# Moving the second-last group's store from the GpSimd queue to the SP queue

## The chip, the cores and the metric

The kernel runs on one core of a Trainium2 chip. The metric is device time in microseconds, as the median of several executions; lower is better. A kernel counts as faster or slower here when it moves by more than 2%.

## The reference, cut to what matters

```python
batch, heads, seq, dim = 8, 12, 512, 64          # Q, K, V float32
Q_feat = np.maximum(0, Q) + 1
K_feat = np.maximum(0, K) + 1
KV = np.einsum('bhkd,bhkv->bhdv', K_feat, V)
K_sum = np.sum(K_feat, axis=2)
numerator = np.einsum('bhqd,bhdv->bhqv', Q_feat, KV)
denominator = np.einsum('bhqd,bhd->bhq', Q_feat, K_sum)
return numerator / (denominator[:, :, :, None] + 1e-10)
```

Three inputs and one output of 12.58 MB each: 50.33 MB have to cross between HBM and the core.

Of the kernel before, what the change touches and what calls it, by code (L numbers as in the profile page):

```python
# [20 lines left out]
def kernel(  # L21
# [23 lines left out]
    NG = NPAIR // NP  # L45
# [57 lines left out]
    def store(g):  # L103
        o_sb = outs.pop(g)
        o_to = o_dram[:, g * NP : g * NP + NP]
        if g < NG - 1:
            nc.gpsimd.dma_start(out=o_to, in_=o_sb)  # L107
            return
        for h in range(2):
            nc.sync.dma_start(out=o_to[:, h:NP:2], in_=o_sb[:, h:NP:2])  # L110
# [83 lines left out]
    with tc.manual_schedule():  # L194
# [36 lines left out]
        for g in range(NG - 1):  # L231
            if g:
                k_features(g)
                q_features(g)
                transposes(g - 1)
            if g >= 2:
                output(g - 2)
            keys_values(g)
            if g + AHEAD < NG:
                load_k(g + AHEAD)  # L240
                load_v(g + AHEAD)
                load_q(g + AHEAD)
            if g >= LAG:
                store(g - LAG)
# [9 lines left out]
        for g in range(last - LAG, NG):  # L254
            store(g)
# [30 lines left out]
```

## The kernel before: the parts the change touches

The work is cut into `NG = 12` groups. For each group the kernel loads K, V (in four pieces) and Q over the GpSimd queue, with a cast from float32 to bfloat16, and stores one output tile of 1 MB. `h` counts the two halves in which a group's output is computed; each half covers every second of the four blocks of the tile.

```python
def store(g):
    o_sb = outs.pop(g)
    o_to = o_dram[:, g * NP : g * NP + NP]
    if g < NG - 1:
        nc.gpsimd.dma_start(out=o_to, in_=o_sb)
        return
    for h in range(2):
        nc.sync.dma_start(out=o_to[:, h:NP:2], in_=o_sb[:, h:NP:2])
# ... (cut: loads, features, matmuls, output)
for g in range(NG - 1):
    # ... (cut: compute of the groups, loads three groups ahead)
    if g >= LAG:                      # LAG = 3
        store(g - LAG)
last = NG - 1
# ... (cut: compute of the last groups)
for g in range(last - LAG, NG):       # groups 8, 9, 10, 11
    store(g)
```

## Time and profile before

| | before |
|---|---|
| time, median of 3 runs | 129.26 us (129.12 to 129.71) |
| span in the profile | 127.4 us |
| busy: PE, DVE, GpSimd, ACT | 57%, 52%, 43%, 37% |
| DMA engines | full from about 3 us to 123 us |
| HBM traffic | 50.33 MB, 395 GB/s over the span |

No compute engine is near its limit, while the DMA engines have no gap. The page's part on DMA issues tells how deep the queue is. Its columns are what is moved, the issuing queue, the count, the size of each, and the median time from issue to landing in us:

```profile
out_dram<-o_sb POOLq DMA_DIRECT2D x11, 1024.0 KB, 12.0
...
out_dram<-o_sb SPq DMA_DIRECT2D x2, 512.0 KB, 5.9
```

A store of 1 MB needs about 2.6 us on 16 engines, yet lands 12.0 us after its issue. Most of the other 9 us it waits behind older transfers.

### The profile page before, as it was taken

The page shows a single profiled execution, that of the slowest core. Times are in us where ns is not written, and L with a number is a line of the kernel's source. Part 1 is how long each engine was busy: PE and PEld are TensorE (multiplying, and loading weights), DVE is VectorE, ACT ScalarE, POOL GpSimd, SP SyncE. Part 2 cuts the span into 40 slices and gives each one's busy share as a digit, 9 for nine tenths or more (in the row PEclk, how much of TensorE's full clock was granted, in tenths as well). Part 3 has the DMA queues.
Part 4 walks back from the last instruction along what each step waited for, and adds up shares of the span by engine and source line. Part 5 has one row for each costly group of instructions (what it writes and reads, how often), then busy time and mean ns, then how long its engine had stood idle before and what let it go on. Part 6 is the DMA issues. An engine that isn't in the chain of part 4 may idle for free.

```text
span 127.4 us, 2373 instructions
## 1 busy us (share of the span) xinstructions
PE 72.6 (57%) x960; PEld 53.0 (42%) x960; DVE 66.1 (52%) x155; ACT 47.1 (37%) x76; POOL 54.3 (43%) x92
## 2 busy tenths in 40 slices
PE   0000099819259691994903992991993896956000
PEld 0000077618146471674702661771662664834000
DVE  4898802086292855919309507705714825779300
ACT  7940006942800927055550054046028009190000
POOL 6695775617346164544442462282273240202000
PEclk9999999999986999599996577568559559996555
DMA  4999999999999999999999999999999999999980
GB/s 89 329 210 210 207 205 208 211 210 208 211 206 214 206 210 214 206 328 256 208 292 293 206 268 321 206 242 344 210 222 353 220 209 371 421 412 421 403 327 2
DMA packets 13914, 32.13 MB, mean 252 GB/s; under 512 B 1360, under 2 KB 1360, under 8 KB 13904
## 3 DMA queue, kind: packets, MB, share of 16 engines
q0 software_dynamic: 13088, 29.89, 99.6%
q1 hardware_dynamic: 816, 2.10, 4.7%
q8 instruction: 7, 0.11, 0.3%
q14 instruction: 3, 0.02, 0.0%
HBM read 37.75 MB, written 12.58 MB: 395 GB/s over the span
## 4 chain that ended last, share of the span: by engine, by line
DMA 61%; DVE 12%; PE 8%; POOL 7%; issue 5%; POOLq 0%
DMA q_raw<-in_Q_dram 33%; DMA k_raw<-in_K_dram 18%; DMA out_dram<-o_sb 10%; DVE o_sb L184 9%; PE kva_ps L141 5%; POOL v_blk L93 5%; PE qt_ps L160 2%; DVE recip L183 2%; PE o_ps L173 1%; POOL q_raw L100 1%; DVE qf L116 1%; POOL k_raw L86 1%; DVE kf L116 1%; POOL zero L195 0%; POOLq L93 0%
## 5 line engine op out<-in xcount | busy, mean ns | idle before, releaser
L141 PE MATMUL kva_ps<-v_blk,kf 128*64 128x320 bf16 x384 | 41.5, 390 | 15.7 <-DMA v_blk<-in_V_dram 15.7
L141 PEld LDWEIGHTS <-kf 128*64 128x64 bf16 x384 | 28.1, 145 | 25.0 <-DVE qf L116 15.7
L173 PE MATMUL o_ps<-kva_diag,qt 128*64 128x130 bf16 x384 | 20.9, 249 | 29.8 <-DVE o_sb L184 29.2
L93 POOL DMA_DIRECT2D v_blk<-in_V_dram x48 | 26.5, 556 | 26.4 <-DMA k_raw<-in_K_dram 12.8
L184 DVE TENSOR_TENSOR o_sb<-o_ps,recip 128x512 f32<-128x512 f32 x48 | 33.2, 691 | 1.6
L151 ACT CAST kva_diag<-kva_ps 64x256 bf16<-64x256 f32 x24 | 8.9, 372 | 66.2 <-PE kva_ps L141 65.9
L161 ACT COPY qt<-qt_ps 128x1024 bf16<-128x1024 bf16 x24 | 29.6, 1301 | 0.3
L173 PEld LDWEIGHTS <-qt 128*64 128x64 bf16 x384 | 13.8, 122 | 35.7 <-DVE o_sb L184 33.9
L116 DVE TENSOR_SCALAR qf<-q_raw 128x1024 bf16<-128x1024 bf16 x24 | 9.2, 426 | 33.6 <-DMA q_raw<-in_Q_dram 33.6
L107 POOL DMA_DIRECT2D out_dram<-o_sb x11 | 8.5, 771 | 22.5 <-DMA q_raw<-in_Q_dram 8.2
L116 DVE TENSOR_SCALAR kf<-k_raw 128x1024 bf16<-128x1024 bf16 (+1 forms) x24 | 10.9, 495 | 9.8 <-DMA k_raw<-in_K_dram 9.8
L160 PE MATMUL qt_ps<-identity,qf 128*128 128x128 bf16 x192 | 13.8, 229 | 0.0
L160 PEld LDWEIGHTS <-qf 128*128 128x128 bf16 x192 | 11.8, 103 | 4.2 <-issue 4.0
L183 DVE RECIPROCAL recip<-o_ps 128x8 f32<-128x8 f32 x48 | 9.5, 197 | 5.2 <-PE o_ps L173 5.2
L86 POOL DMA_DIRECT2D k_raw<-in_K_dram x11 | 7.8, 713 | 8.5 <-DVE recip L183 5.2
L100 POOL DMA_DIRECT2D q_raw<-in_Q_dram x12 | 8.8, 730 | 4.6 <-DMA v_blk<-in_V_dram 2.1
L152 ACT CAST kva_diag<-kva_ps 64x4 bf16<-64x4 f32 x24 | 4.0, 168 | 0.0
L206 DVE MEMSET v_blk<- 128x2925 f32 x1 | 2.5, 2496 | 0.7 <-DVE ones L202 0.7
L224 DVE MEMSET v_blk<- 128x2925 f32 x1 | 2.5, 2496 | 0.6 <-issue 0.6
L212 DVE MEMSET v_blk<- 128x2925 f32 x1 | 2.5, 2496 | 0.6 <-issue 0.6
L219 POOL MEMSET kva_diag<- 128x520 bf16 x3 | 2.0, 719 | 0.0
L207 ACT COPY v_blk<-zero 128x2195 f32<-128x2195 f32 x1 | 2.0, 2019 | 0.0
(15 smaller groups left out, 7.9 us busy)
## 6 DMA issues: line engine op xcount, KB each, us to landing
out_dram<-o_sb POOLq DMA_DIRECT2D x11, 1024.0 KB, 12.0
q_raw<-in_Q_dram POOLq DMA_DIRECT2D x12, 512.0 KB, 10.8
v_blk<-in_V_dram POOLq DMA_DIRECT2D x48, 128.0 KB, 9.3
k_raw<-in_K_dram POOLq DMA_DIRECT2D x11, 512.0 KB, 11.9
k_raw<-in_K_dram SPq DMA_DIRECT2D x1, 1024.0 KB, 4.9
out_dram<-o_sb SPq DMA_DIRECT2D x2, 512.0 KB, 5.9
```

The source lines that it names most:

```text
L86: (nc.sync if g == 0 else nc.gpsimd).dma_start(out=k_raw, in_=k_dram[:, g * 2 : g * 2 + 2])
L93: nc.gpsimd.dma_start(out=v_blk[g % NV][32 * b : 32 * b + 32, b], in_=v_dram[32 * b : 32 * b + 32, 2 * g : 2 * g + 2],)
L100: nc.gpsimd.dma_start(out=q_raw, in_=q_dram[:, g * 2 : g * 2 + 2])
L107: nc.gpsimd.dma_start(out=o_to, in_=o_sb)
L116: nc.vector.tensor_scalar(out=dst, in0=src, scalar1=1.0, scalar2=1.0, op0=ALU.add, op1=ALU.max)
L141: nc.tensor.matmul(kva_ps[64 * n : 64 * n + 64], lhsT=kf[:, c, n, :], rhs=vb[:, :, n, c, :], start=(c == 0), stop=(c == C2 - 1),)
L151: nc.scalar.copy(out=kva[ps, :, n, 0:D], in_=kva_ps[ps, 0:4, :])
L160: nc.tensor.transpose(qt_ps[:, c, :], qf[:, half * C + c, :, :], identity)
L161: nc.scalar.copy(out=qt[:, :, :, half], in_=qt_ps)
L173: nc.tensor.matmul(ops[c // 4][64 * j : 64 * j + 64, c // 2 % 2, (c % 2) * W : (c % 2) * W + W], lhsT=qt[:, c, 32 * b : 32 * b + 32, :], r ...
L183: nc.vector.reciprocal(out=recip, in_=cells[:, :, :, :, D:D1])
L184: nc.vector.tensor_tensor(out=o_sb[:, h:NP:2, 4 * i : 4 * i + 4].rearrange("p n (b c) d -> p b c n d", b=2), in0=cells[:, :, :, :, 0:D], i ...
```

## The change

The intent: let the group before the last be stored like the last one, in halves that leave as soon as they are computed, over SP's queue.

```diff
     def store(g):
         o_sb = outs.pop(g)
         o_to = o_dram[:, g * NP : g * NP + NP]
-        if g < NG - 1:
+        if g < NG - 2:
             nc.gpsimd.dma_start(out=o_to, in_=o_sb)
             return
         for h in range(2):
```

## The prediction

> **What bounds the kernel now.** I read the page's slices first. DMA engines stand at 9 from the second slice to the third from the end, while PE is at 57% of the span and DVE at 52%. The rate row needs one remark: loads convert float32 to bfloat16 on the way, so a slice full of loads shows some 208 GB/s written for 416 read, and the stores at the end show 403 to 421. It is the same rate all along.
>
> ```profile
> DMA  4999999999999999999999999999999999999980
> GB/s 89 329 210 210 207 205 208 211 210 208 211 206 214 206 210 214 206 328 256 208 292 293 206 268 321 206 242 344 210 222 353 220 209 371 421 412 421 403 327 2
> ...
> HBM read 37.75 MB, written 12.58 MB: 395 GB/s over the span
> ```
>
> So 50.33 MB move at about 414 GB/s, which is 121.6 us by itself, beside about 3 us of start (a slow first slice) and about 3 us of end. Nothing in the middle can be won by moving work between engines; only the end, after the last byte, is short of transfers.
>
> The second view is the table of stretches over that end. Its last two numbers are DMA share and GB/s.
>
> ```profile
> 112.00:116.00 4.00, 1.93 (x44) 1.31 (x42) 3.52 (x10) 2.40 (x2) 0.00 (x0) 0.96 1.03 416
> 116.00:120.00 4.00, 1.75 (x24) 1.02 (x20) 3.01 (x7) 0.00 (x0) 0.75 (x1) 0.50 1.02 413
> ...
> 120.00:124.00 4.00, 0.00 (x0) 0.00 (x0) 0.00 (x0) 0.00 (x0) 0.00 (x0) 0.50 0.92 355
> 124.00:128.00 4.00, 0.00 (x0) 0.00 (x0) 0.00 (x0) 0.00 (x0) 0.00 (x0) 0.50 0.02 7
> ```
>
> The reader is to see two things. Compute ends at 119.1, yet transfers fill the engines to past 123: the stores have piled up behind the loads. And between about 124.5 and 127.4 nothing at all moves. Those 2.9 us belong to no transfer and to no counted instruction.
>
> What happens in them is in the third view, the instructions of the program's end (L281), with minimum/median/maximum ns and first and last start:
>
> ```profile
> L281 SPq EVENT_SEMAPHORE  x9: 17/28/3544, 119.6 to 127.3; - x9
> L281 POOLq EVENT_SEMAPHORE  x4: 17/17/17, 126.7 to 127.3; - x4
> L281 POOLq DRAIN  x3: 51/102/10595, 116.0 to 127.1; - x3
> L281 SPq DRAIN  x3: 7/7/7, 124.9 to 126.9; - x3
> ```
>
> SP waits for every DMA one after the other and reaches its DRAIN at 124.9, when the last store has landed. GpSimd's first DRAIN starts at 116.0, right at its last DMA issue (116.05), and takes 10,595 ns: it ends at 126.63. Only then does GpSimd's next semaphore instruction run (126.7), and all other engines are released behind it. SP was ready at 124.95, so **the GpSimd drain holds the end for about 1.7 us**. The page's chain of waits doesn't show it, because these instructions count as no work: its last piece is the DVE multiply at 118.42.
>
> **What the Trainium skill says.** "DMA: Bandwidth & Descriptors", section "Issuing engines are not separate DMA queues": all issuing engines share the same 16 DMA engines, so another issuer saves only issue time. The trace agrees: at 116 to 120, with a GpSimd store and two SP stores issued, the rate is 413 GB/s, no more than the 416 before. So the change cannot win bandwidth.
>
> The same page, "Queues, rings and completion order", says an engine takes packets of its queue rows in turn. The trace shows it only in part: the first SP half is issued at 117.47, its first packet runs at 119.5, and most of its packets from 120.5, when the fast DMA engines are through with most of the GpSimd backlog.
>
> "Perfetto Trace Analysis", section "DMA Instruction — SWDGE (GPSIMD)": the instruction's end is the end of descriptor generation, not of the movement. The trace agrees: 0.75 us for the last GpSimd store, 7.2 us to its landing.
>
> "VectorE: DVE Perf Modes", section "The DRAIN you can't avoid", calls the other DRAINs boilerplate of about 12 ns, constant on all engines. Here the trace differs: SP's take 7 ns, GpSimd's last long one 10,595 ns. That no page says what it waits for is the main uncertainty.
>
> **The change part by part.** The instruction order of the two kernels differs in one thing: GpSimd has five stores after the last load instead of six, SP has four half stores instead of two. PE, DVE and ACT are unchanged.
>
> *Issue.* Removed: one GpSimd issue, 0.75 us, at 116.05. Added: two SP issues of about 0.38 us. None is on the path; SP waits 116.4 us for its first store today.
>
> *Start of group 10's store.* Its first half is complete at 114.08 (second multiply of that group's output) and its second at 115.77. It could be issued at about 114.1 instead of 116.05, 1.95 us earlier. **Worth nothing**: the DMA share is 1.03 and 1.02 in the two stretches from 112 to 120, and the store of group 9, issued at 110.25, lands only at 119.85. An earlier place in a queue that never runs dry doesn't move the end.
>
> *Packets.* The DMA view of 113 to 127 gives what a store costs on each queue:
>
> ```profile
> q0 software_dynamic: 861, 3.29, 58.0%
> q1 hardware_dynamic: 544, 1.05, 19.7%
> ```
>
> The columns are packets, MB, share of 16 engines over 14 us. GpSimd's queue: 0.580 x 14 = 8.12 us per engine for 3.29 MB, or 2.59 us for the 1.05 MB of one group. SP's queue: 0.197 x 14 = 2.76 us for the same amount. The SP packets are 2 KB (82 to 88 ns each in the trace), the GpSimd store's are 4 KB (159 ns). Moving one group's store therefore adds 2.76 - 2.59 = **+0.17 us** of engine time, in the saturated stretch, so on the path.
>
> *The drain.* The last GpSimd transfer lands at 116.05 + 7.2 = 123.23; the drain ends at 126.63, 3.40 us later. I choose the reading that the drain waits until GpSimd's own transfers are finished and cleared. With the change its last transfer is group 9's, which lands at 119.85 today. The SP halves of group 10 come in from about 116 on and may be served in turn with it, at most 32 packets of 84 ns = 2.7 us. So landing is 119.85 to 122.55 and the drain ends at 123.25 to 125.95, middle 124.6.
>
> *Sum.* SP's last landing 124.81 + 0.17 = 124.98; SP's DRAIN done at 124.95 + 0.17 = 125.12; that is later than the drain's middle, so SP now ends the kernel. From drain end to the end of the span the trace has 127.39 - 126.63 = 0.76. Span: 125.12 + 0.76 = 125.88. The timed run of that profile was 129.16 for a span of 127.39, 1.77 outside; and the median of the runs, 129.26, is 0.10 above it. 125.88 + 1.77 + 0.10 = 127.75, say **127.8**: 1.5 us less, 1.1%.
>
> **The rivals.**
>
> 1. *The drain is not tied to GpSimd's transfers* (it ends some time after the last transfer of any queue, or is a fixed cost of the end). For it: the drain's end is also 1.8 us after the last SP landing, and one trace can't separate the two. Against it: GpSimd has no part in the SP stores, and its DRAIN carries no semaphore; at the start of the program, with no transfer out, its DRAIN took 0.18 us. Then only the packets count: 129.26 + 0.17 = 129.4. I give it about one in four.
>
> 2. *The SP queue becomes the bound.* Four half stores wait together, and the later ones might be held back until the first have left, with the 2 us from issue to first packet then in the open. For it: that delay of 119.5 - 117.47. Against: group 10's halves are ahead by 1.7 us each, the backlog to feed the engines lasts past 119, and each of the two SP issues today took under 0.39 us with no sign of a full queue. It would cost up to 1 us of the gain: 128.3 to 128.8.
>
> 3. *The transfers end sooner because the work is spread better.* Half of the DMA engines are done at 123.5, the others at 124.8 (landings of the last store go from 123.44 to 124.81). If the halves ran first where engines lag, up to 0.7 us more: about 127.1. Against: every store goes to the same engines in equal shares, and the spread is already 1.3 to 1.8 us in nearly every transfer since 52.
>
> **Range and chances.** With weights of about 0.65 for the main reading, 0.25 for rival 1 and 0.1 for the others, the times lie at 127.8, 129.4 and 127.1 to 128.8. The range 127.2 to 129.5 holds both main outcomes. Two per cent faster means under 126.68, 1.1 us below my number: more than the packets, the drain and rival 3 together give, so 0.04. Slower by 2% would take 131.8, for which nothing speaks: 0.01. Within 2%: 0.95.
>
> **What would show it.** In the profile after: the GpSimd DRAIN should be over before SP's, so between 123 and 125.2, about 3.4 us after GpSimd's last landing; the next GpSimd semaphore instruction should start within 0.1 us of SP's DRAIN, near 125.15, where today the distance is 1.7 us. SP's queue should show about 1,088 packets in that stretch and about 39% of 14 us. SP's last landing should be at 124.8 to 125.2; if it is earlier than 124.6, the claim that an earlier issue is worth nothing is wrong. DMA share should stay at 1.0 to about 123; a dip between 118 and 122 would be rival 2. If the drain still ends 1.7 us or more after SP's DRAIN, rival 1 is right and the time is near 129.4.

## The result, and the profile after

| | before | after |
|---|---|---|
| time, median of 4 runs | 129.19 us (128.96 to 129.71) | 127.66 us (127.56 to 128.12) |
| ratio of fast runs | 1 | 0.9883 (95%: 0.9844 to 0.9922) |
| span in the profile | 127.4 us | 126.0 us |
| last GpSimd landing | 123.23 | 121.33 |
| GpSimd drain ends | 126.63 | 124.69 |
| last SP landing | 124.81 | 125.06 |
| SP's second DRAIN ends | 124.95 | 125.20 |
| GpSimd's next semaphore instruction | 126.67 | 125.23 |

All runs were fast. A ratio here and below is the ratio of fast runs, with its 95% interval; it is not quite the ratio of the medians. The landings are the times at which the last of a transfer's 16 semaphore increments is recorded. The gain is 1.5 us, 1.2%: within the 2% band, as forecast.

The instructions of the program's end in the changed kernel (minimum/median/maximum ns, then first and last start in us):

```profile
L281 POOLq EVENT_SEMAPHORE  x4: 17/17/17, 125.2 to 125.9; - x4
L281 POOLq DRAIN  x3: 51/101/15532, 109.2 to 125.7; - x3
L281 SPq DRAIN  x3: 7/7/7, 125.1 to 125.4; - x3
```

The long GpSimd DRAIN starts earlier, at 109.2, because GpSimd's last issue is now group 9's. It lasts longer, 15,532 ns, and still ends earlier: 109.16 + 15.53 = 124.69. A long duration in this line is therefore no cost by itself; the end of it is what counts. SP's DRAIN comes at 125.1, after it, and GpSimd's semaphore instruction follows 0.03 us behind SP, where before it came 1.7 us behind.

The stretches of the end (last two numbers: DMA share, GB/s):

```profile
112.00:116.00 4.00, 2.46 (x40) 1.68 (x40) 3.83 (x11) 1.34 (x2) 0.00 (x0) 0.75 1.03 418
116.00:120.00 4.00, 0.95 (x14) 0.47 (x10) 2.05 (x5) 0.00 (x0) 0.00 (x0) 0.50 1.02 411
120.00:124.00 4.00, 0.00 (x0) 0.00 (x0) 0.00 (x0) 0.00 (x0) 0.00 (x0) 0.50 0.95 366
124.00:128.00 4.00, 0.00 (x0) 0.00 (x0) 0.00 (x0) 0.00 (x0) 0.00 (x0) 0.50 0.03 12
```

The transfers look as before: full to 120, 0.95 and 0.03 after. They did not end sooner; the silence behind them became shorter.

The queues between 113 and 127 us (packets, MB, share of 16 engines):

```profile
q0 software_dynamic: 610, 2.31, 40.5%
q1 hardware_dynamic: 1088, 2.10, 38.8%
```

SP's two groups take 0.388 x 14 / 2 = 2.72 us of every engine each. GpSimd's queue takes 0.405 x 14 = 5.67 us for 2.31 MB, or 2.57 us for the 1.05 MB of one group. The extra cost of SP's smaller packets is 0.15 us for a group.

### The profile page after: what moved, and what is told of

Its sections match the earlier page's. It is cut to its first block, busy times and chain, and to the rows that moved or that the text cites. A ratio compares the mean times of both kernels' runs of the same rounds, so it can differ in the third digit from the quotient of the medians.

```text
span 126.0 us, 2374 instructions
## 1 busy us (share of the span) xinstructions
PE 69.4 (55%) x960; PEld 51.1 (41%) x960; DVE 66.3 (53%) x155; ACT 47.1 (37%) x76; POOL 53.4 (42%) x91
## 4 chain that ended last, share of the span: by engine, by line
DMA 67%; DVE 9%; PE 8%; POOL 6%; issue 4%; POOLq 0%
DMA k_raw<-in_K_dram 25%; DMA q_raw<-in_Q_dram 17%; DMA v_blk<-in_V_dram 16%; DMA out_dram<-o_sb 9%; DVE o_sb L184 7%; PE kva_ps L141 5%; POOL v_blk L93 4%; POOL q_raw L100 2%; PE qt_ps L160 2%; DVE recip L183 1%; PE o_ps L173 1%; DVE qf L116 1%; POOL k_raw L86 1%; POOL zero L195 0%; POOLq L100 0%
## 5 line engine op out<-in xcount | busy, mean ns | idle before, releaser
L141 PE MATMUL kva_ps<-v_blk,kf 128*64 128x320 bf16 x384 | 40.6, 385 | 15.8 <-DMA v_blk<-in_V_dram 15.8
L173 PE MATMUL o_ps<-kva_diag,qt 128*64 128x130 bf16 x384 | 19.1, 234 | 32.0 <-DVE o_sb L184 31.3
L184 DVE TENSOR_TENSOR o_sb<-o_ps,recip 128x512 f32<-128x512 f32 x48 | 33.2, 691 | 1.6
L173 PEld LDWEIGHTS <-qt 128*64 128x64 bf16 x384 | 12.7, 114 | 37.5 <-DVE o_sb L184 35.8
L107 POOL DMA_DIRECT2D out_dram<-o_sb x10 | 7.7, 774 | 16.1 <-DMA q_raw<-in_Q_dram 7.8
L160 PE MATMUL qt_ps<-identity,qf 128*128 128x128 bf16 x192 | 13.1, 223 | 0.0
L160 PEld LDWEIGHTS <-qf 128*128 128x128 bf16 x192 | 11.1, 99 | 3.4 <-issue 3.2
```

The source lines that it names most:

```text
L141: nc.tensor.matmul(kva_ps[64 * n : 64 * n + 64], lhsT=kf[:, c, n, :], rhs=vb[:, :, n, c, :], start=(c == 0), stop=(c == C2 - 1),)
L160: nc.tensor.transpose(qt_ps[:, c, :], qf[:, half * C + c, :, :], identity)
L173: nc.tensor.matmul(ops[c // 4][64 * j : 64 * j + 64, c // 2 % 2, (c % 2) * W : (c % 2) * W + W], lhsT=qt[:, c, 32 * b : 32 * b + 32, :], r ...
L184: nc.vector.tensor_tensor(out=o_sb[:, h:NP:2, 4 * i : 4 * i + 4].rearrange("p n (b c) d -> p b c n d", b=2), in0=cells[:, :, :, :, 0:D], i ...
```

## The experiments

Two theories were to be told apart first. **Drain theory**: the kernel ends behind the later of two things, the GpSimd drain, some 3.4 us after GpSimd's last landing, and SP's DRAIN, 0.13 us after SP's last landing. **Start theory**: the gain comes from the earlier start of group 10's store, or from the SP queue moving it better. The diffs below are shortened; they stand against the changed kernel, those of e3 and of the last four runs against the kernel before.

### e1_whole_sp: on SP, but as one late store

```diff
+        if g == NG - 2:
+            nc.sync.dma_start(out=o_to, in_=o_sb)
+            return
```

> Group 10 goes over SP, but as one whole store, issued at about 115.8 instead of 114.1 for its first half. Drain theory (the end is the later of: last GpSimd landing + 3.4, last SP landing + 0.13; then 0.77 to the end of the span and 1.77 outside it): nothing is lost by the later issue, the GpSimd drain ends near 124.5, SP's DRAIN near 125.1, time 127.6 to 127.8. Rival (the gain of the change is the earlier start of group 10's store): most of it is given back, 128.9 to 129.2.

Measured: 127.96 us against 129.75 for before on the same chip, ratio 0.9876 (0.9837 to 0.9916). The whole gain is there although the store was issued at 114.56 instead of in halves from 113.04.

```profile
L284 POOLq DRAIN  x3: 51/96/14768, 109.0 to 125.6; - x3
L284 SPq DRAIN  x3: 7/7/7, 125.1 to 125.4; - x3
```

The drain ended at 109.00 + 14.77 = 123.76, SP's DRAIN came at 125.1. The drain ended earlier than I wrote (123.76 for "near 124.5"), because GpSimd's last landing was already at 120.41; the lag was 3.36. The halves are not what gained.

### e2_halves_pool: in halves, but on GpSimd

```diff
+        queue = nc.gpsimd if g == NG - 2 else nc.sync
         for h in range(2):
-            nc.sync.dma_start(...)
+            queue.dma_start(...)
```

> Group 10 in halves and early, but on the GpSimd queue. Drain theory: the last GpSimd landing stays near 123.2, the drain ends near 126.6, time 129.1 to 129.4, no gain. Rival (earlier start): the gain is there without SP, 127.6 to 127.9.

Measured: 129.93 us against 129.75, ratio 1.0041 (0.9993 to 1.009). (One of the four runs is slow; the three fast ones have a mean of 129.47 against 129.63 for before, so there is no clear gain either way.) Group 10's first half was issued at 112.94, as early as in the changed kernel, and nothing was won. In the profile, which fell on the fastest of the runs (128.55), SP was ready at 124.69 and the GpSimd drain ended at 126.02, 3.44 us after the last GpSimd landing at 122.58:

```profile
L282 POOLq DRAIN  x3: 51/102/11423, 114.6 to 126.5; - x3
L282 SPq DRAIN  x3: 7/7/7, 124.6 to 126.3; - x3
```

Together with e1 this is the cross of the two parts of the change: queue without early start wins, early start without queue does not.

### e7_late_ten: on SP in halves, but issued last of all

```diff
-        for g in range(last - LAG, NG):
+        for g in [*range(last - LAG, NG - 2), NG - 1, NG - 2]:
             store(g)
```

> The changed kernel with group 10's two halves issued last, after group 11's, so at about 119 instead of 114.1 and 115.8, five and three us later. Drain theory: the queues still hold work when they are issued, or run dry for well under 1 us; 127.7 to 128.3. Rival (start of group 10's store matters): later than before's 116.05 by 3 us, so 129.3 to 131.

Measured: 127.89 us against 129.61, ratio 0.9889 (0.9803 to 0.9976). Group 10's halves were issued at 119.48 and 120.00, more than five us later than in the changed kernel, and the last SP landing was at 125.15 instead of 125.06. The queues did thin out for a moment (share 0.85 from 118 to 120), and yet, between these two traces, the earlier place was worth only 0.1 us.

```profile
L281 POOLq DRAIN  x3: 51/101/13309, 110.2 to 125.8; - x3
L281 SPq DRAIN  x3: 7/7/7, 125.2 to 125.5; - x3
```

The long drain ended at 110.15 + 13.31 = 123.46. This trace also removes a rival that the profile of the changed kernel leaves: there compute happened to end about 1 us earlier than before (last multiply from 117.43, before from 118.42). In e7 it ended as late as before, and the span was still 126.1 us.

### e4_small_late_pool: 64 KB late on GpSimd

```diff
         for h in range(2):
+            end = 112 if g == NG - 1 and h == 1 else P
-            nc.sync.dma_start(out=o_to[:, h:NP:2], in_=o_sb[:, h:NP:2])
+            nc.sync.dma_start(out=o_to[:end, h:NP:2], in_=o_sb[:end, h:NP:2])
+            if end < P:
+                nc.gpsimd.dma_start(out=o_to[end:, h:NP:2], in_=o_sb[end:, h:NP:2])
```

> The changed kernel, but 16 of the 128 partitions of the very last half store (64 KB, half a per cent of the output) go over GpSimd. Drain theory: the drain now waits for this late piece, landing near 124.9, and ends near 128.3; time 130.5 to 131.0, worse than before by over 1 us. Rival (early start or the SP queue's handling of the bulk made the gain): the bulk is unchanged, 127.6 to 128.0.

Measured: three runs at 131.80 to 132.06 us and one at 129.13; the three are over 1.5% above the fastest of the same kernel, so no ratio is given. The one fast run fits neither forecast, so the times decide nothing here. The trace, of one of the three, shows the mechanism:

```profile
L284 POOLq DRAIN  x3: 46/101/11408, 118.1 to 130.0; - x3
L284 SPq DRAIN  x3: 7/7/7, 126.8 to 129.8; - x3
```

GpSimd's small piece landed at 126.11 and the drain ended at 118.10 + 11.41 = 129.51, 3.40 us later and 2.6 us after SP was ready. One part of this is not the drain: 15 of the piece's 16 increments had come by 124.42 and the last one came 1.7 us later. Why it was late, and why one run was 2.7 us shorter, stays open; the short run has no trace.

### e3_all_pool: every store on GpSimd, where the theory failed

```diff
-        if g < NG - 1:
-            nc.gpsimd.dma_start(out=o_to, in_=o_sb)
-            return
-        for h in range(2):
-            nc.sync.dma_start(...)
+        nc.gpsimd.dma_start(out=o_to, in_=o_sb)
```

> All stores over GpSimd, the last too. Drain theory: the last GpSimd landing is the last of all, at about 124.5, the drain ends at about 127.9, span 128.7, time 130.2 to 130.7: slower than before although the bytes and the packets (4 KB) are if anything cheaper. Rival (the end is the last landing of any queue plus a fixed time, 2.6 us as before): span 127.1, time 128.9 to 129.3.

Measured: 128.63 us against 129.75, ratio 0.9901 (0.9847 to 0.9955): *shorter* than before by 1% (within the 2% band), where the drain theory with its constant lag wanted 130.2 to 130.7. The end and the GpSimd timeline of this run:

```profile
L277 POOLq DRAIN  x3: 51/95/5428, 120.7 to 126.7; - x3
L277 SPq DRAIN  x3: 7/7/7, 126.2 to 126.5; - x3
```

```profile
115.54 0.75 POOL L106 DMA_DIRECT2D out_dram<-o_sb  x1 [5.05 <-DVE recip L179]
120.76 0.76 POOL L106 DMA_DIRECT2D out_dram<-o_sb  x1 [4.47 <-issue]
```

Two things are new. The drain ended at 120.74 + 5.43 = 126.17, only **0.38 us** after the last GpSimd landing at 125.79. And group 11's store, whose data was complete at 118.62 (the last increment of DVE's semaphore), was issued at 120.76. The timeline gives "issue" for that wait, which means that it knows no releaser. The engines, full until 121, then ran dry: the share of the stretch 121 to 122 was 0.57. My reading is that something that usually follows the last landing was done here ahead of the last store; the trace doesn't name it.

### e5_three_sp, e6_four_sp, e8_all_sp: more stores on SP

```diff
-        if g < NG - 2:        # e5: NG - 3, e6: NG - 4, e8: no store on GpSimd
```

> Groups 9, 10 and 11 over SP in halves. Drain theory: the drain already lies before SP's DRAIN in the changed kernel, so nothing more is won; the drain ends 3.4 us after the last GpSimd landing (now group 8's, about 117.5 to 119), so about 121 to 122.5, well before SP's DRAIN at about 125.4; one more group in 2 KB packets costs 0.17 us: 127.7 to 128.0. Rival (each group moved to SP wins by its earlier start): 126.2 to 127.

> Groups 8 to 11 over SP. Measures the drain by itself: the last GpSimd transfer is then group 7's store, landing about 115. Drain theory, lag a constant of the end: drain over at about 118.4. If the drain instead needs the last transfers of any queue, it ends past 124 as always. Time: 2 x 0.17 us over the changed kernel, 127.8 to 128.2.

> All twelve groups' stores over SP in halves; GpSimd carries loads alone. Measures the packets: ten more groups in 2 KB packets at 0.17 us each, 127.66 + 1.7 = 129.4 (128.8 to 129.8), with the drain far off the path (last GpSimd landing is a load near 108 to 112). If the packets cost nothing in total: 127.7.

Measured: 128.64, 128.52 and 135.41 us against 129.61, ratios 0.9927 (0.9866 to 0.9989), 0.9914 (0.9849 to 0.9979) and 1.0465 (1.0386 to 1.0544). The start theory wanted 126 to 127 for e5, so it fails again. But all three are also slower than I wrote, each for another reason.

In e5 the wait that names the loss is this one (who waited for what: total us, times, longest):

```profile
DVE o_sb L184 <- DMA out_dram<-o_sb: 4.4, 1, 4.4
```

DVE's first multiply of the last output stood still until 120.00, when the second half of group 9, issued by SP at 109.73, had landed at 119.88. Group 11's stores could then leave only at 121.56 and 123.24, with the queues dry. The trace has the wait as an instruction of DVE (L184, until 119.96) on two semaphores, those of the two half stores of group 9. So the program itself makes the last output tile wait for group 9's store; why it pairs these two, with six output buffers, is not settled.

In e6 the last GpSimd transfer, group 7's store, was issued at 102.33 and landed at 120.49, not near 115: it had to share the engines with SP's halves for 18 us. The lag behind it was 3.28 us, and the drain, done at 123.77, was off the path; my landing was wrong. That doesn't explain the time. The loss is at SP, whose last landing, 125.13, was as early as in the changed kernel:

```profile
L281 SPq DRAIN  x3: 7/7/7, 125.6 to 125.9; - x3
```

SP checks the DMA semaphores one after the other, in a fixed order, 0.06 us each. In the changed kernel the last half's semaphore comes last, and the second DRAIN ends 0.15 us after the landing. In e6 it comes third, seven more checks follow, and the second DRAIN ends at 125.70, 0.57 us after the landing. That is 0.43 us of the 0.51 us by which this span is longer. (In e8 the distance is 0.57 us too.) So the 0.13 us of the drain theory is not a constant either.

In e8 the same sharing hit the loads. The last load landed at 119.45 (before: 107.17), and compute came after it, with the engines partly idle:

```profile
120.00:124.00 4.00, 3.20 (x58) 2.47 (x56) 2.28 (x6) 2.28 (x6) 0.00 (x0) 1.00 0.66 254
124.00:126.00 2.00, 1.06 (x24) 0.74 (x24) 1.90 (x6) 1.05 (x1) 0.00 (x0) 1.00 0.19 74
```

Shares of 0.66 and 0.19 are to be seen there, about 3 us of idle engines, where the changed kernel is full to 120. Stores that wait behind earlier loads on GpSimd's queue were here served between them: a load of Q landed 14.1 us after its issue at the median (before: 10.8). The packets cost more as well: SP's took 96 ns at the median in this trace, 84 in the changed kernel, and the twelve stores 35.3 us of every engine, against 31.0 in the changed kernel, so 0.43 us for each of the ten groups moved and not 0.17. The kernel became 5.8 us longer; the runs don't divide this between the idle engines and the packets.

### The second theory: the drain's length counts transfers

The lags of the ten profiles so far are not one constant with noise. Sorted by the number of GpSimd transfers in the program they lie on a line, with e3 alone beside it. "Descriptors" is a count per DMA engine from the packet records of GpSimd's queue: one for each completion, one for each 2 KB row, so a 4 KB packet counts two. That weight is a choice of mine, to which I come back below.

| run | GpSimd transfers | descriptors | last GpSimd landing | drain ends | lag us |
|---|---|---|---|---|---|
| e8_all_sp | 71 | 631 | 119.45 | 122.40 | 2.95 |
| e6_four_sp | 79 | 895 | 120.49 | 123.77 | 3.28 |
| e5_three_sp | 80 | 928 | 119.97 | 123.29 | 3.32 |
| after, e1, e7 | 81 | 961 | 121.33, 120.41, 120.10 | 124.69, 123.76, 123.46 | 3.36 each |
| before | 82 | 994 | 123.23 | 126.63 | 3.40 |
| e4_small_late_pool | 82 | 964 | 126.11 | 129.51 | 3.40 |
| e2_halves_pool | 83 | 995 | 122.58 | 126.02 | 3.44 |
| e3_all_pool | 83 | 1027 | 125.79 | 126.17 | **0.38** |

The slope is (3.44 - 2.95) / (83 - 71) = 0.041 us for each transfer, and 3.40 - 82 x 0.041 leaves 0.04 us. Before and e4 differ by 30 descriptors and have the same lag, so transfers count, not descriptors. For e3, which has as many transfers as e2, I supposed that a ring of descriptors (a list of fixed length that is filled again from its start) had come round and that the pass over the old transfers had been made there. Four more runs tested this with tiny loads of 256 bytes, whose data nobody uses:

```diff
# ... (cut: the tile scratch; f3 has the same lines in the changed kernel, f4 in e3's)
+            if 1 <= g < 5:      # 12 of them; 9: 24 of them
+                for i in range(12 * g - 12, 12 * g, 4):
+                    nc.gpsimd.dma_start(
+                        out=scratch[0:16, i : i + 4], in_=q_dram[0:16, 0, 0, 0:4]
+                    )
             if g >= LAG:
                 store(g - LAG)
```

> The kernel before plus 12 tiny useless GpSimd loads (256 bytes each, in the middle of the kernel): 94 GpSimd transfers instead of 82. Count theory, from ten profiles (the drain ends 0.05 us + 0.0408 us x the number of GpSimd transfers after GpSimd's last landing; 71 give 2.95, 83 give 3.44): lag 3.88 us, 0.48 more than before, time 129.6 to 130.0. Rival (the lag is a constant of about 3.4 that just happened to drift): 3.40.

> The kernel before plus 24 of the same: 106 transfers, 1042 descriptors per DMA engine on the GpSimd queue (before 994, 1018 with 12 more; the run with all stores on GpSimd had 1027 and a lag of 0.38). Plain count theory: lag 4.38, time 130.1 to 130.6. Count with a reset (when a ring of about 1024 descriptors comes round, the pass over the old transfers is made there, in the middle of the backlog, and the drain has only the rest): lag under 1.2 us, drain no longer last, time 127.5 to 128.2, over 1 us FASTER than before although work was added.

> The changed kernel plus the 24 tiny loads: 105 transfers, 1009 descriptors per engine, so no coming round. Count theory: lag 4.34; with the last GpSimd landing near 121.3 the drain ends near 125.6, 0.4 us after SP's DRAIN, and holds the end again: 127.9 to 128.5. With a reset at a count of transfers (over 83 or so) instead of descriptors: lag under 1.2, 127.6 to 127.9. With a constant lag: 3.36, 127.6 to 127.9.

> All stores on GpSimd and the 24 tiny loads: 1075 descriptors per engine, so the ring comes round at group 10's store or before, hidden in the backlog, and not at group 11's as in the run with all stores on GpSimd, where it kept that store back by 2 us (issue at 120.76, ready at 118.62). Count with a reset: last store issued near 118.8, last landing near 124.6, lag under 1.5 us, time 127.0 to 127.9 without any store on SP. If the stall of 2 us has another cause, it is still there: 128.3 to 128.9. Plain count: lag 4.4, 131 or more.

| run | GpSimd transfers | descriptors | lag us | time us | before, same chip |
|---|---|---|---|---|---|
| f1_before_12_more | 94 | 1018 | 3.89 | 132.91 | 129.30 |
| f2_before_24_more | 106 | 1042 | 0.37 | 132.07 | 129.30 |
| f3_after_24_more | 105 | 1009 | 4.67 | 133.50 | 129.30 |
| f4_all_pool_24_more | 107 | 1075 | 0.41 | 132.80 | 129.30 |

The times are medians of all runs, slow ones too. **The lags came out as written in f1, f2 and f4; the times did not.** In f1 the lag was 3.89 for a forecast of 3.88, which a constant or a drift does not give. In f2 and f4 it collapsed, as in e3. The ends of f1 and f2, f1 first:

```profile
L287 POOLq DRAIN  x3: 51/102/12865, 116.4 to 129.8; - x3
L287 SPq DRAIN  x3: 7/7/7, 127.1 to 129.6; - x3
```

```profile
L287 POOLq DRAIN  x3: 51/102/9580, 119.8 to 129.9; - x3
L287 SPq DRAIN  x3: 7/7/7, 129.3 to 129.6; - x3
```

In f1 GpSimd drained to 116.43 + 12.87 = 129.30, 2.2 us behind SP's DRAIN at 127.13. In f2 it was done at 119.79 + 9.58 = 129.37, with SP's DRAIN at 129.36, although it had 12 transfers more. (The profile of f2 is of a run called slow; the lag is a distance within one trace.)

The times missed because the tiny loads were not free: in f1 the last SP landing moved from 124.81 to 126.99, in f2 to 129.19. I took their bytes for their cost. Where in the middle they cost it was not looked into. So the "faster than before by added work" that f2 was to show was not shown; f2 was 1.1% longer, ratio 1.011 (1.0026 to 1.0193, from only two fast runs of six), within the 2% band. f1 and f4 have 1.0241 (1.0171 to 1.0312 and 1.019 to 1.0292): longer, but whether by more than 2% is unclear. In f4 the last store was issued at 122.66, with its data complete at 122.36, and not near 118.8 as I had written.

f3 gave no usable time with its profile: the profiled run, a slow one, took 203.56 us, because TensorE took twice as long (792 ns for a matmul into `kva_ps` at the mean, 385 in the changed kernel), for a reason that I don't know. GpSimd's issues of V were not stretched (551 ns, 552 there), and the lag is again a distance within one trace:

```profile
L287 POOLq DRAIN  x3: 51/101/9420, 179.5 to 201.5; - x3
```

GpSimd's last landing was at 184.22 and the drain ended at 179.47 + 9.42 = 188.89, so the lag was 4.67 us. A constant wanted 3.36 and a reset at a count of transfers under 1.2, and both fail; the count wanted 4.34, and why this lag is 0.33 us longer stays open. The three other runs took 132.13 to 133.84 us, ratio 1.0279 (1.0216 to 1.0343), slower; no trace tells how much of that is the drain and how much the tiny loads.

The pass has a price where it is made, too. In e3 one store was kept back by 120.76 - 118.62 = 2.14 us with 82 transfers before it. In f2 and f4 it was group 10's store, issued at 119.81 and 121.68 with data complete at 117.13 and 119.00: 2.68 us in both, with 105 transfers before it. That is 0.026 us for each transfer in all three (0.023 without the 0.28 us that lie between complete data and issue in the kernel before as well, 115.77 to 116.05). It fits a pass over old transfers, but what exactly sets it off is argued from three runs with 1027 to 1075 descriptors and the others with at most 1018. The border depends on the weight of the 4 KB packets: counted as they stand in the trace, e3 with its short lag has 835 packets for each engine, and f1 and f3 with their long ones 842 and 849. A ring that comes round in between is the reading I have, not one that a run has isolated.

No run beats the changed kernel clearly: e1 and e7 have its ratio within the noise.

## Why the prediction was right

**Where the time could come from.** The prediction's mechanism held as well as its number. The step "only the end, after the last byte, is short of transfers" holds. The DMA share is 1.03 and 1.02 between 112 and 120 in both kernels, and the whole gain lies behind the last landing.

**Early start worth nothing.** Right. Issued in halves at 113.0 and 114.7 (changed kernel), whole at 114.6 (e1) or at 119.5 and 120.0 (e7), group 10 gave the same time within 0.3 us, though e1 and e7 were not timed side by side with the changed kernel, so it is the ratios to before that are compared: 0.9883, 0.9876, 0.9889.

**Packets, +0.17 us.** About right: 0.15 us by the queue's shares, 0.25 us by the last SP landing (124.81 to 125.06), which also has the spread between executions in it.

**The drain.** Predicted to end between 123.25 and 125.95, middle 124.6, and to be no longer the last; it ended at 124.69, 0.5 us before SP's DRAIN. That it lies so near the middle is luck: the range was 2.7 us wide, and in its upper 0.8 us the drain would still have ended after SP's DRAIN (125.12 in the sum). Predicted lag 3.40 us, measured 3.36. The span came to 125.97 for a forecast of 125.88, the time to 127.66 for 127.75 in the sum.

**What was chosen and not known.** I took the lag for a constant of a drain that waits for GpSimd's own transfers and clears them. The waiting is shown: the drain follows GpSimd's last landing in all these profiles, whatever SP does. The constant is not: from 71 to 94 transfers the lag is 0.041 us for each GpSimd transfer of the program. It made no difference here because the change removes one transfer of 82, so 0.04 us. In e3 neither the constant nor the count holds, because the lag collapsed; that forecast was wrong by 1.6 to 2.1 us. The prediction also set GpSimd's DRAIN against the skill's 12 ns; that comparison doesn't hold, as the last section says.

**The rivals.** Rival 1, a drain tied to the last transfer of any queue, would have ended it behind 125.06; it ended at 124.69, and at 123.46 in e7. Rival 2, SP's queue as the bound, is not seen: four halves were under way together, each issue took 0.37 to 0.38 us, and no stretch dips before 120. Rival 3, a better spread over the engines, is not seen either: the landings of the last half spread over 1.97 us (before: 1.37), so somewhat worse.

## What to carry to other kernels

When a kernel ends on stores, look at what the engines do after the last byte: a drain on the queue's owner can hold the end although every transfer is done, and the chain of waits doesn't show it. Here it helped to let another queue carry the last transfers, just so many that the drain of the first queue is over when they land, and no more, because a second queue used all along delayed the loads and had costlier packets (e8: 4.6% slower). And a lag that looks like a constant in one trace should be plotted against what the program does many times before it is put into a sum.

## What the Trainium skill lacked or had wrong

- "VectorE: DVE Perf Modes", section "The DRAIN you can't avoid", gives about 12 ns, on all engines, for the DRAINs that the runtime puts before and after a program. The DRAINs here stand on a line of the kernel file (L281), so the page isn't shown to be wrong; it lacks this kind. GpSimd's at the end of the program lasts until its last transfer has landed and then another 2.95 to 3.89 us: 0.041 us for each GpSimd transfer of the program (71 to 94 of them; 4.67 us with 105 in f3), or 0.37 to 0.41 us in three runs with more than 1018 descriptors for each DMA engine. I found no page that has this.
- I found no page with the stall of a GpSimd issue that goes with those short drains: 2.14 us with 82 transfers before it, 2.68 us with 105.
- "DMA: Bandwidth & Descriptors", section "Issuing engines are not separate DMA queues", says that a second issuer only saves issue time. For bandwidth that agrees (in the changed kernel 411 GB/s at 116 to 120 with both queues moving data, 418 just before with GpSimd's alone), but the choice of the queue moved the end by 1.5 us through the drain, and with all stores moved the kernel was 5.8 us longer, its loads of Q landing after 14.1 us and not 10.8.
- The same page, section "SWDGE vs HWDGE vs iDMA", gives up to 4096 B as a packet's preferred size, in its table of the path from GpSimd. That agrees: GpSimd's stores of 2 KB rows went as 4 KB packets of 159 ns. What SP's stores do isn't there: those of the same rows, whole or in halves, went as 2 KB packets of 84 ns at the median: 0.15 us more for 1.05 MB.
